# A two-layer transformer step in fp32: the first layer's modulation products move from VectorE to TensorE, and x is loaded first

## The chip, the cores and the metric

The kernel runs on one core of a Trainium2 chip. The metric is the device time of one execution in microseconds (us); the time of a kernel is the median over several runs. TensorE (PE) does matrix products, VectorE (DVE) and ScalarE (ACT) elementwise work and reductions, GpSimd (POOL) a few small powers, and SyncE (SP) issues the loads and stores.

## The reference, cut to what matters

The model has two layers, each with an attention half and an MLP half. Two streams of 128 tokens (context and latent) pass through the same weights; the model width is 2048. A conditioning vector per stream gives six vectors of 2048 per layer (shift, scale and gate of either half), and shift and scale have to be known before the first product of a half.

```python
def modulation(cvec, w_ada_l, b_ada_l):
    m = jax.nn.silu(cvec) @ w_ada_l + b_ada_l          # 2048 x 12288 weights per layer
    return jnp.split(m[:, None, :], N_MOD, axis=-1)

for l in range(DEPTH):                                  # DEPTH = 2
    sh_a, sc_a, gt_a, sh_m, sc_m, gt_m = modulation(...)
    h = rms_norm(x, g_pre_a) * (1.0 + sc_a) + sh_a
    o = attention(h @ w_in[l]) @ w_out[l]               # w_in 2048 x 4608, w_out 2048 x 2048
    x = x + gt_a * rms_norm(o, g_post_a)
    h = rms_norm(x, g_pre_m) * (1.0 + sc_m) + sh_m
    x = x + gt_m * rms_norm(jnp.square(jax.nn.relu(h @ w_up[l])) @ w_down[l], g_post_m)
```

## The kernel before

All weights stream once from HBM through SBUF, in tiles of 128 x 2048 fp32 (1 MB) called `raw`. There are five `raw` buffers (`NRAW`), and SP loads the tiles in the order in which they are used, each as soon as a buffer is free. There are three sorts of tiles:

- **Trunk tiles** (`w_in`, `w_out`, `w_up`, `w_down`). Each is split in two halves into a rounded high part `wh` (ACT, line 988) and the rest `wl` (DVE, line 989), at most three half tiles ahead (`NW`). TensorE then makes three products (`wh`·high x, `wl`·high x, `wh`·low x) per piece, 24 matmuls of 512 columns per tile of `w_in` or `w_out` (`Group.run`, lines 346 to 348).
- **Modulation tiles on TensorE** (`w_ada`, `ada_mm`, line 135). One block is one section (0 shift, 1 scale, 2 gate of the attention half; 3, 4, 5 of the MLP half) and 512 features, in four tiles. Each tile is four matmuls with 32 columns of weights. After the fourth, ACT copies the result out (`pt`, line 139), TensorE transposes it in four pieces, and DVE finishes it (`ada_post`, `mod_fin`, `gate_fin`).
- **Modulation tiles on DVE** (`w_adaT`, `dv_mul`, line 189). The transposed weights are multiplied with the broadcast conditioning vectors `sB`, one instruction for each of the two streams, with the sum in the instruction's accumulator. `load_sb` loads `sB`.

`M_A` are the eight blocks of shift and scale of the attention half, `M_M` those of the MLP half, `G_A` and `G_M` the four gate blocks of each. `DV_BLOCKS` and `PE_BLOCKS` say which engine makes which. In the first layer DVE makes `G_A`, the first two of `M_M` and `G_M` (the last in the MLP half); TensorE makes the rest.

The first layer starts with no modulation at hand. Its input product is therefore done in four **quarters** f = 0 to 3 of the 2048 input features: `make_xt(0, 0, f)` normalises, transposes, scales and shifts 512 features into `XT[f]` (high and low part), and then the `w_in` tiles of these features run for four groups of outputs ("34", "56", "78", "01"), two tiles each. Each group's sums leave PSUM after each quarter, the first time by ACT (line 776), later by DVE adding onto `stg` (line 778). The modulation of the next quarter (eight `w_ada` tiles) is woven between them, and so are some DVE tiles. Then come four tiles of the last group "2" (`c2`), the attention, and 16 tiles of `w_out`, with the rest of the modulation woven in. The attention units (`gqa`, `diff`, `na`) are stepped along between the half tiles and run to their end where a `w_out` tile needs their result.

What the code emits in this order goes through a scheduler, which sets the final order of each engine's instructions; each engine then works through its list strictly in order. `startup` loads constants on ACT's queue; `pre_norm_first` loads x on SP's queue, behind the first eight modulation tiles, and makes the row norms.

## Time and profile before

| | |
|---|---|
| median of 3 runs | 2423.8 us (2419.22 to 2427.26) |
| the profiled execution | 2420.71 us, span 2418.6 us |
| PE busy | 2301.6 us, 95% of the span |
| DVE busy | 1704.7 us, 70% |
| ACT busy | 1096.0 us, 45% |
| moved by DMA | 601.32 MB, mean 249 GB/s |
| granted TensorE clock, mean | 0.973 of full speed |

Busy time counts the union of an engine's instructions; matmuls overlap, so an engine that reads 95% can still have waited. In a chain of waits every piece is what the end waited for at that time. In a table of stretches the numbers behind the length are the busy times of PE, its weight loads, DVE, ACT and POOL with the number of instructions, then the granted clock as a share of 2.4 GHz, the share of the DMA engines' time in use, and the GB/s moved.

### The profile page before, as it was taken

The page shows a single profiled execution, that of the slowest core. Times are in us where ns is not written, and L with a number is a line of the kernel's source. Part 1 is how long each engine was busy: PE and PEld are TensorE (multiplying, and loading weights), DVE is VectorE, ACT ScalarE, POOL GpSimd, SP SyncE. Part 2 cuts the span into 40 slices and gives each one's busy share as a digit, 9 for nine tenths or more (in the row PEclk, how much of TensorE's full clock was granted, in tenths as well). Part 3 has the DMA queues.
Part 4 walks back from the last instruction along what each step waited for, and adds up shares of the span by engine and source line. Part 5 has one row for each costly group of instructions (what it writes and reads, how often), then busy time and mean ns, then how long its engine had stood idle before and what let it go on. Part 6 is the DMA issues. An engine that isn't in the chain of part 4 may idle for free.

```text
span 2418.6 us, 32541 instructions
## 1 busy us (share of the span) xinstructions
PE 2301.6 (95%) x13200; PEld 1915.8 (79%) x13200; DVE 1704.7 (70%) x2093; ACT 1096.0 (45%) x1514; POOL 33.2 (1%) x30
## 2 busy tenths in 40 slices
PE   6978988889999999999998999999999999999998
PEld 3656665659989989989976777776988988988986
DVE  2557898559888888989857687646665666565545
ACT  3523343445445434434445455546544543543543
POOL 0000000000000000000000010000000000000000
PEclk8989997999999999999998999999999999999999
DMA  9877686666777777777855766666655655665552
GB/s 366 297 304 315 252 322 232 236 265 249 293 284 292 290 284 268 290 295 282 315 221 187 265 222 235 248 223 227 225 207 212 225 208 210 215 221 209 179 187 87
DMA packets 91342, 601.32 MB, mean 249 GB/s; under 512 B 13624, under 2 KB 16056, under 8 KB 19256
## 3 DMA queue, kind: packets, MB, share of 16 engines
q1 hardware_dynamic: 90472, 598.64, 66.7%
q8 instruction: 103, 1.69, 0.3%
q10 hardware_dynamic: 720, 0.61, 0.1%
q14 instruction: 47, 0.39, 0.0%
HBM read 591.61 MB, written 7.60 MB: 248 GB/s over the span
## 4 chain that ended last, share of the span: by engine, by line
PE 87%; DVE 6%; DMA 2%; issue 2%; ACT 2%; POOL 1%; ACTq 0%; POOLq 0%; DVEq 0%
PE acc L346 17%; PE acc L347 17%; PE acc L348 17%; PE acc L382 9%; PE acc L381 9%; PE acc L380 9%; PE ada L135 2%; PE m L111 2%; DVE wl L989 2%; DVE junk L189 1%; POOL st L108 1%; DVE raw L189 1%; PE m L217 1%; DMA ngT<-ngT_in 1%; PE m L468 1%
## 5 line engine op out<-in xcount | busy, mean ns | idle before, releaser
L989 DVE TENSOR_TENSOR wl<-raw,wh 128x1024 fp32r<-128x1024 f32 x720 | 875.3, 1222 | 462.7 <-ACT wh L988 459.6
L988 ACT ACTIVATE wh<-raw 128x1024 fp32r<-128x1024 f32 x720 | 760.0, 1059 | 967.1 <-PE acc L348 592.3
L380 PE MATMUL acc<-XT,wh 128*128 128x256 f32 x2048 | 578.5, 283 | 2.8 <-ACT XT L261 2.8
L382 PE MATMUL acc<-XT,wl 128*128 128x256 f32 x2048 | 579.4, 283 | 1.6 <-DVE wl L989 1.5
L381 PE MATMUL acc<-XT,wh 128*128 128x256 f32 x2048 | 578.1, 282 | 0.3 <-DVE XT L262 0.3
L347 PE MATMUL acc<-wl,big 128*128 128x512 f32 x1280 | 509.8, 398 | 1.0 <-DVE wl L989 1.0
L346 PE MATMUL acc<-wh,big 128*128 128x512 f32 x1280 | 508.7, 401 | 1.8 <-ACT wh L988 1.8
L348 PE MATMUL acc<-wh,big 128*128 128x512 f32 x1280 | 507.6, 397 | 0.0
L380 PEld LDWEIGHTS acc<-XT,wh 128*128 128x128 f32 x2048 | 387.2, 189 | 4.3 <-ACT XT L261 3.5
L382 PEld LDWEIGHTS acc<-XT,wl 128*128 128x128 f32 x2048 | 386.7, 189 | 3.0 <-DVE wl L989 2.8
L381 PEld LDWEIGHTS acc<-XT,wh 128*128 128x128 f32 x2048 | 387.3, 189 | 1.1 <-DVE XT L262 0.8
L346 PEld LDWEIGHTS acc<-wh,big 128*128 128x128 f32 x1280 | 241.9, 189 | 68.4 <-issue 8.1
L347 PEld LDWEIGHTS acc<-wl,big 128*128 128x128 f32 x1280 | 242.9, 190 | 58.6 <-DVE wl L989 3.3
L348 PEld LDWEIGHTS acc<-wh,big 128*128 128x128 f32 x1280 | 242.7, 190 | 57.4 <-issue 1.7
L189 DVE SCALAR_TENSOR_TENSOR junk<-raw,sB 128x2048 fp8e5<-128x2048 f32 x116 | 265.1, 2285 | 32.2 <-DMA raw<-w_adaT_in 32.1
L189 DVE SCALAR_TENSOR_TENSOR raw<-raw,sB 128x2048 f32<-128x2048 f32 x116 | 264.9, 2284 | 0.1
L346 PE MATMUL acc<-wh,XT 128*128 128x512 f32 x576 | 236.0, 417 | 25.5 <-ACT XT L261 18.6
L347 PE MATMUL acc<-wl,XT 128*128 128x512 f32 x576 | 235.5, 410 | 9.5 <-DVE wl L989 9.3
L348 PE MATMUL acc<-wh,XT 128*128 128x512 f32 x576 | 232.5, 406 | 0.3 <-DVE XT L262 0.3
L346 PEld LDWEIGHTS acc<-wh,XT 128*128 128x128 f32 x576 | 111.7, 195 | 67.1 <-ACT XT L261 20.7
L347 PEld LDWEIGHTS acc<-wl,XT 128*128 128x128 f32 x576 | 112.7, 196 | 40.2 <-DVE wl L989 15.1
L348 PEld LDWEIGHTS acc<-wh,XT 128*128 128x128 f32 x576 | 111.9, 195 | 26.5 <-DVE XT L262 1.5
(132 smaller groups left out, 1200.9 us busy)
## 6 DMA issues: line engine op xcount, KB each, us to landing
raw<-w_up_in SPq DMA_DIRECT2D x128, 1024.0 KB, 4.9
raw<-w_down_in SPq DMA_DIRECT2D x128, 1024.0 KB, 4.9
raw<-w_adaT_in SPq DMA_DIRECT2D x116, 1024.0 KB, 4.9
raw<-w_in_in SPq DMA_DIRECT2D x72, 1024.0 KB, 5.9
raw<-w_ada_in SPq DMA_DIRECT2D x64, 1024.0 KB, 6.7
raw<-w_out_in SPq DMA_DIRECT2D x32, 1024.0 KB, 5.0
XT<-w_ada_in SPq DMA_DIRECT2D x12, 1024.0 KB, 6.9
sB<-crow_in SPq DMA_DIRECT2D x2, 1024.0 KB, 13.8
```

The lines of the kernel that those rows point to most:

```text
L108: pool.tensor_tensor(out, out, hf[:, 0:width], ALU.pow)
L111: pe.transpose(out, in_, ident)
L135: pe.matmul(pa[32 * g:32 * g + 32, :], sT[:, 4 * kq + g, :], raw[:, g * 512:(g + 1) * 512], start=(kq == 0), stop=(kq == 3), tile_position ...
L189: dve.scalar_tensor_tensor(o, raw, 1.0, sB[v], ALU.mult, ALU.mult, accum_out=a[:, j, v:v + 1], saturate=None if v else False)
L346: pe.matmul(a, xh, wh[:, c], start=first, stop=False)
L347: pe.matmul(a, xh, wl[:, c], start=False, stop=False)
L348: pe.matmul(a, xl, wh[:, c], start=False, stop=last)
L380: pe.matmul(a, wh[:, c], xh, start=first, stop=False)
L381: pe.matmul(a, wh[:, c], xl, start=False, stop=False)
L382: pe.matmul(a, wl[:, c], xh, start=False, stop=last)
L988: act.activation(wh, r, AF.Copy)
L989: dve.tensor_tensor(wl, r, wh.bitcast(F32), ALU.subtract)
```

## The change

1. In the first layer only `G_M` stays on DVE. `G_A` and the first two blocks of `M_M`, six blocks or 24 tiles, become `w_ada` tiles on TensorE. Nothing runs as a DVE product before the first layer's MLP half; `load_sb` moves there in the code.
2. x is loaded by `startup`, as the first thing on SP's queue.
3. The first two blocks (shift and scale of the first 512 features) are cut in halves of 256 features; a tile is then 128 x 1024 (0.5 MB, new array `w_ada0`). `make_xt` can make half a quarter, and the first `w_in` tiles run on it.
4. The four groups get five PSUM segments with bounds 0, 2, 4, 8, 12, 16 (in 128-feature steps) in place of four of equal size: one more addition of each sum onto `stg`.
5. `make_xt` of the next quarter is called ahead of the last three `w_in` tiles of the present one, and the eight modulation tiles go between its first five.

```diff
-DV_BLOCKS = [G_A + M_M[:2] + G_M, M_A + M_M[:4] + G_A[:3] + G_M]
-PE_BLOCKS = [M_A + M_M[2:], M_M[4:] + G_A[3:]]
+DV_BLOCKS = [G_M, M_A + M_M[:4] + G_A[:3] + G_M]
+PE_BLOCKS = [M_A[2:] + G_A + M_M, M_M[4:] + G_A[3:]]
...
     def startup():
+        for s in range(2):
+            x[s] = sb([P, D], "big", 5)
+            nc.sync.dma_start(x[s], xd[s])
...
-    def ada_mm(l, sec, blk, kq, raw):
+    def ada_mm(l, sec, blk, kq, raw, half=None):
+        w = 512 if half is None else 256
...
-            pe.matmul(pa[32 * g:32 * g + 32, :], sT[:, 4 * kq + g, :], raw[:, g * 512:(g + 1) * 512],
+            pe.matmul(pa[32 * g:32 * g + 32, 0:w], sT[:, 4 * kq + g, :], raw[:, g * w:(g + 1) * w],
...
-    def make_xt(l, w, f):
+    def make_xt(l, w, f, j0=0, j1=4):
...
     def pre_norm_first():
         nt[0] = sb([P, 4, 512], "big", 5)
-        for s in range(2):
-            x[s] = sb([P, D], "big", 5)
-            nc.sync.dma_start(x[s], xd[s])
...
-        def stg_done(key, ntile, after=None, S=S, nseg=4 if l == 0 else 1):
+        def stg_done(key, ntile, after=None, S=S, nseg=5 if l == 0 else 1):
...
-        gr = [Group(2, KT, xl, stg_done(key, 2, after[key]), 4 if l == 0 else None) for key in after]
+        gr = [Group(2, KT, xl, stg_done(key, 2, after[key]), [0, 2, 4, 8, 12, 16] if l == 0 else None) for key in after]
...
-            fill = ada_items(0, M_M[2:])
-            dv = dv_items(0, G_A + M_M[:2])
-            a0 = ada_items(0, M_A[:2])
-            items.extend(a0[:3])
+            fill, dv = ada_items(0, G_A + M_M), []
+            h0 = lambda h: [("ada", I["w_ada0"][sec, h, kq], (0, sec, 0, kq, h)) for sec in range(2) for kq in range(4)]
+            items.extend(h0(0)[:2])
             call(pre_norm_first)
-            items.extend(a0[3:])
-            for f in range(4):
-                call(lambda f=f: (drain_fast(), make_xt(0, 0, f)))
+            items.extend(h0(0)[2:])
+            xt = lambda *a: call(lambda: (drain_fast(), make_xt(0, 0, *a)))
+            xt(0, 0, 2)
+            m = [cg[0] for cg in cG] + [cg[1] for cg in cG]
+            ah, a1 = h0(1), ada_items(0, M_A[2:4])
+            items.extend(m[:1] + ah[:4] + m[1:2] + ah[4:] + m[2:3])
+            xt(0, 2, 4)
+            items.extend(a1[:2] + m[3:4] + a1[2:4] + m[4:5] + a1[4:6] + m[5:6] + a1[6:] + m[6:7])
+            xt(1)
+            items.extend(m[7:])
+            for f in range(1, 4):
                 ch = [c for cg in cG for c in cg[2 * f:2 * f + 2]]
-                if f == 0:
-                    ch.insert(4, ("call", load_sb))
...
                 if f < 3:
-                    weave(ch, ada_items(0, M_A[2 * f + 2:2 * f + 4]), dv[:3] if f else ())
-                    dv = dv[3:] if f else dv
+                    weave(ch[:5], ada_items(0, M_A[2 * f + 2:2 * f + 4]))
+                    items.append(ch[5])
+                    xt(f + 1)
+                    items.extend(ch[6:])
                 else:
-                    weave(ch, fill[:4], dv[:6])
-            weave(c2, fill[4:6], dv[6:10])
-            rest, fill, dv = [], fill[6:], dv[10:]
+                    weave(ch, fill[:8])
+            weave(c2, fill[8:16])
+            rest, fill = [], fill[16:]
...
-        cut = 8 if l == 0 else 40
+        cut = 0 if l == 0 else 40
...
         if l + 1 < L:
+            rest.insert(1, ("call", load_sb))
             g, m = dv_items(0, G_M), dv_items(1, M_A + M_M[:4])
...
-            weave(rest[2:118], [], dv)
+            weave(rest[4:119], [], dv)
```

At the start, SP's queue of the kernel before (`big` is x):

```order
L975 DMA raw<-w_ada_in 128x2048 x8
L268 DMA big<-xp_in 128x2048
L268 DMA big<-xs_in 128x2048
L975 DMA raw<-w_in_in 128x2048 x2
L975 DMA raw<-w_ada_in 128x2048 x2
```

and of the changed kernel:

```order
L116 DMA big<-xp_in 128x2048
L116 DMA big<-xs_in 128x2048
L988 DMA raw<-w_ada_in 128x1024 x8
L988 DMA raw<-w_in_in 128x2048
L988 DMA raw<-w_ada_in 128x1024 x4
L988 DMA raw<-w_in_in 128x2048
```

The first `w_in` tile stands behind two x tiles and eight half tiles (6 MB), where it stood behind 10 MB.

DVE's list of the kernel before where the second quarter hands over to the third (`st_88` is the sum of a modulation block, `mod` its result, `XT_105` the third quarter's input, `junk` and `raw` the two halves of a DVE product):

```order
L152 TENSOR_REDUCE st_88<-m 128x8
L189 SCALAR_TENSOR_TENSOR junk,aacc<-raw,sB_89 128x2048
L168 SCALAR_TENSOR_TENSOR mod_0_75<-st_88,baT 128x4 x2
L189 SCALAR_TENSOR_TENSOR raw,aacc<-raw,sB_90 128x2048
L169 TENSOR_TENSOR mod_0_75<-mod_0_75,ngT 128x4 x2
L989 TENSOR_TENSOR wl<-raw,wh 128x1024
L254 TENSOR_SCALAR big<-m,mod_0_75,mod_1_76 128x128 x4
L262 TENSOR_TENSOR XT_105<-big,XT_105 128x4x128
```

and of the changed kernel at the same place (the third quarter's input is `XT_109` there):

```order
L157 TENSOR_REDUCE st_88<-m 128x8
L174 SCALAR_TENSOR_TENSOR mod_0_75<-st_88,baT 128x4 x2
L175 TENSOR_TENSOR mod_0_75<-mod_0_75,ngT 128x4
L248 TENSOR_SCALAR big<-big,st_139 128x512
L1002 TENSOR_TENSOR wl<-raw,wh 128x1024 x2
L175 TENSOR_TENSOR mod_0_75<-mod_0_75,ngT 128x4
L259 TENSOR_SCALAR big<-m,mod_0_75,mod_1_76 128x128 x2
L1002 TENSOR_TENSOR wl<-raw,wh 128x1024
L782 TENSOR_TENSOR stg<-stg,acc 128x512 x4
L1002 TENSOR_TENSOR wl<-raw,wh 128x1024
L259 TENSOR_SCALAR big<-m,mod_0_75,mod_1_76 128x128 x2
L267 TENSOR_TENSOR XT_109<-big,XT_109 128x4x128
```

The two DVE products between the modulation's steps are gone, and splits and additions of tiles that still belong to the present quarter stand there.

TensorE's list of the kernel before during `w_out`, where the normed output of `diff` for the first stream (`tmp`) is transposed:

```order
L346 MATMUL acc<-wh,big 128x512
L347 MATMUL acc<-wl,big 128x512
L348 MATMUL acc<-wh,big 128x512
L111 MATMUL m<-cs,tmp 128x128 x2
L607 MATMUL m<-kT,qT 128x256
L111 MATMUL m<-cs,tmp 128x128 x2
```

and of the changed kernel:

```order
L349 MATMUL acc<-wh,big 128x512
L350 MATMUL acc<-wl,big 128x512
L351 MATMUL acc<-wh,big 128x512
L140 MATMUL ada<-raw,sT 32x512 x8
L111 MATMUL m<-cs,tmp 128x128 x3
L611 MATMUL m<-kT,qT 128x256
```

Two modulation tiles (eight matmuls) now stand ahead of the transposes, on the engine that waits there.

## Rows read from the trace of the kernel before

**Rows 1.** Stretches: length; busy PE, PEld, DVE, ACT, POOL; clock, DMA share, GB/s.

```profile
0.00:34.80 34.80, 13.38 (x76) 3.42 (x76) 4.79 (x24) 9.74 (x25) 1.36 (x6) 0.88 0.95 389
34.80:96.80 62.00, 58.05 (x277) 41.35 (x278) 24.75 (x35) 35.45 (x49) 0.09 (x1) 0.96 0.87 349
96.80:174.80 78.00, 64.44 (x274) 42.96 (x274) 54.73 (x73) 25.37 (x33) 0.00 (x0) 0.90 0.80 286
174.80:243.90 69.10, 58.39 (x278) 41.86 (x278) 49.29 (x69) 21.05 (x25) 0.00 (x0) 0.92 0.76 303
243.90:304.70 60.80, 58.13 (x258) 41.05 (x258) 50.62 (x78) 21.42 (x35) 4.63 (x2) 0.96 0.68 253
304.70:346.90 42.20, 35.29 (x152) 25.27 (x151) 38.29 (x66) 15.53 (x25) 2.44 (x1) 0.88 0.84 318
346.90:470.80 123.90, 104.67 (x462) 71.33 (x460) 96.19 (x166) 48.06 (x116) 6.02 (x2) 0.85 0.63 229
470.80:522.80 52.00, 52.00 (x237) 38.02 (x236) 23.14 (x32) 21.89 (x32) 0.56 (x1) 1.00 0.77 294
522.80:541.00 18.20, 11.97 (x83) 4.07 (x82) 13.22 (x35) 13.01 (x33) 2.54 (x3) 0.91 0.81 313
541.00:1504.00 963.00, 948.31 (x5656) 825.48 (x5657) 813.10 (x918) 458.31 (x600) 9.30 (x7) 0.99 0.71 266
```

**Rows 2.** Chain of waits at the start: start us, length us, what.

```profile
17.55 9.76 DMA big<-xp_in
...
32.63 0.74 DVE big L254 x2
...
34.81 1.22 PE acc L346 x2
```

**Rows 3.** Timeline of the start and first quarter: start us, length us, engine, line, instruction.

```profile
22.37 1.07 PE L135 MATMUL ada<-raw,sT 128*32 128x512 f32 x8 [1.43 <-DMA raw<-w_ada_in]
...
24.86 1.07 PE L135 MATMUL ada<-raw,sT 128*32 128x512 f32 x8 [1.43 <-DMA raw<-w_ada_in]
...
26.70 1.12 PE L111 MATMUL m<-cs,pt 128*128 128x128 f32 x4 [0.78 <-ACT pt L139]
...
28.28 0.24 DVE L169 TENSOR_TENSOR mod<-mod,ngT 128x4 f32<-128x4 f32 x2
...
45.04 0.39 PE L347 MATMUL acc<-wl,XT 128*128 128x512 f32 x1
...
45.27 0.40 PE L348 MATMUL acc<-wh,XT 128*128 128x512 f32 x1
```

**Rows 4.** Chain of waits from the second to the third quarter.

```profile
167.00 2.21 DVE junk L189 x2
...
169.43 2.06 issue
...
174.85 0.79 PE acc L346
```

**Rows 5.** Waits of PE, 34.8 to 304.7 us: total us, times, longest us.

```profile
PE acc L346 <- ACT XT L261: 15.8, 3, 8.3
```

**Rows 6.** DVE groups, 0 to 541 us: count, busy us, mean ns of one, idle before.

```profile
L189 DVE SCALAR_TENSOR_TENSOR raw<-raw,sB 128x2048 f32<-128x2048 f32 x24 | 54.8, 2284 | 0.1
...
L778 DVE TENSOR_TENSOR stg<-stg,acc 128x512 f32<-128x512 f32 x48 | 32.3, 684 | 27.2 <-PE acc L348 27.0
```

**Rows 7.** Timeline of PE: two modulation tiles in the midst of `w_out` products.

```profile
513.24 1.92 PE L135 MATMUL ada<-raw,sT 128*32 128x512 f32 x16
515.10 1.19 PE L346 MATMUL acc<-wh,big 128*128 128x512 f32 x4
```

**Rows 8.** Chain of waits in `c2`, 304.7 to 346.9 us, shares by line.

```profile
by line: DVE junk L189 15.6%; DVE raw L189 10.5%; PE acc L348 8.6%; DVE wl L989 8.0%; PE acc L347 7.6%; issue 7.1%; PE acc L346 6.9%; POOL st L108 5.8%; PE m L502 4.6%; PE m L111 3.8%; DVE big L451 3.3%; DVE st L421 2.8%; ACT big L450 2.6%;
```

**Rows 9.** Chain of waits during the first `w_out` tiles.

```profile
413.92 4.67 DMA raw<-w_ada_in
...
424.40 2.21 DVE junk L189 x2
```

More of the change, by code (lines that the diff above doesn't have):

```diff
@@ L138, in ada_mm, with ada_post @@
             pt = sb([P, 512], "pt")
-            act.activation(pt, pa, AF.Copy)
-            fast.append(ada_post(l, sec, blk, pt))
+            act.activation(pt[:, 0:w], pa[:, 0:w], AF.Copy)
+            fast.append(ada_post(l, sec, blk, pt, 0 if half is None else 2 * half, w // P))
     gcs = {}
     made = set()
-    def ada_post(l, sec, blk, pt):
+    def ada_post(l, sec, blk, pt, j0, nj):
         yield
         m = psm()
-        for j in range(4):
+        for j in range(nj):
             tr(m[:, j * P:(j + 1) * P], pt[:, j * P:(j + 1) * P])
         yield
-        red = st1[:, 0:8].rearrange("p (j v) -> p j v", v=2)
-        dve.tensor_reduce(red, m.rearrange("p (j g c) -> p j c g", g=4, c=32)[:, :, 0:2, :], AX.X, ALU.add)
+        red = st1[:, 0:2 * nj].rearrange("p (j v) -> p j v", v=2)
+        dve.tensor_reduce(red, m[:, 0:nj * P].rearrange("p (j g c) -> p j c g", g=4, c=32)[:, :, 0:2, :], AX.X,
+                          ALU.add)
         if sec in (2, 5):
@@ L241, in make_xt @@
             if s == 0:
-                dve.tensor_scalar(xn, x[s][:, c], r, None, ALU.mult)
+                dve.tensor_scalar(xn[:, cn], x[s][:, c], r, None, ALU.mult)
             else:
-                act.activation(xn, x[s][:, c], AF.Copy, scale=r)
+                act.activation(xn[:, cn], x[s][:, c], AF.Copy, scale=r)
             m = psm()
-            for j in range(4):
-                k = 4 * f + j
+            for j in range(j0, j1):
                 tr(m[:, j * P:(j + 1) * P], xn[:, j * P:(j + 1) * P])
             step = 2 if f == 0 else 4
-            for j in range(4):
+            for j in range(j0, j1):
                 k = 4 * f + j
@@ L257, in make_xt @@
                 if (j + 1) % step == 0:
-                    j0 = j + 1 - step
-                    tv = t[:, j0 * P:(j + 1) * P].rearrange("p (j q) -> p j q", j=step)
-                    hi = XT[f][:, j0:j + 1, 0, s * P:(s + 1) * P]
+                    i = j + 1 - step
+                    tv = t[:, i * P:(j + 1) * P].rearrange("p (j q) -> p j q", j=step)
+                    hi = XT[f][:, i:j + 1, 0, s * P:(s + 1) * P]
                     act.activation(hi, tv, AF.Copy)
-                    dve.tensor_tensor(XT[f][:, j0:j + 1, 1, s * P:(s + 1) * P], tv, hi.bitcast(F32), ALU.subtract)
+                    dve.tensor_tensor(XT[f][:, i:j + 1, 1, s * P:(s + 1) * P], tv, hi.bitcast(F32), ALU.subtract)
     def pre_norm_first():
         nt[0] = sb([P, 4, 512], "big", 5)
-        for s in range(2):
-            x[s] = sb([P, D], "big", 5)
-            nc.sync.dma_start(x[s], xd[s])
         for s in range(2):
@@ L336, in run @@
                             for _ in range(2)]
-            q, i0 = divmod(self.cnt, self.seg)
-            end = i0 + len(steps) == self.seg
+            q, i0 = self.q, self.cnt - self.segs[self.q]
+            seg = self.segs[q + 1] - self.segs[q]
+            end = i0 + len(steps) == seg
             for s in range(2):
@@ L342, in run @@
                     for i, (kt, wh, wl) in enumerate(steps):
-                        first, last = i0 + i == 0, i0 + i == self.seg - 1
+                        first, last = i0 + i == 0, i0 + i == seg - 1
                         c = slice(n * 512, (n + 1) * 512)
@@ L353, in run @@
                 self.acc = None
+                self.q += 1
         def left(self):
-            return self.seg - self.cnt % self.seg
+            return self.segs[self.q + 1] - self.cnt
     class UpGroup:
@@ L868, in trunk @@
                 rest.append(("call", load))
-        cut = 8 if l == 0 else 40
+        cut = 0 if l == 0 else 40
         nf = (len(fill) - TAIL) * cut // len(rest) // 2 * 2
-        weave(rest[:cut], fill[:nf], dv)
+        if cut:
+            weave(rest[:cut], fill[:nf], dv)
         weave(rest[cut:], fill[nf:], tail=TAIL)
@@ L931, in trunk @@
         if l + 1 < L:
+            rest.insert(1, ("call", load_sb))
             g, m = dv_items(0, G_M), dv_items(1, M_A + M_M[:4])
             dv = [x for i in range(16) for x in m[3 * i:3 * i + 3] + g[i:i + 1]]
-            weave(rest[:2], [])
-            weave(rest[2:118], [], dv)
+            weave(rest[:4], [])
+            weave(rest[4:119], [], dv)
             call(lambda: drain_dv())
             call(lambda l=l: layer_consts(l + 1))
-            items.extend(rest[118:])
+            items.extend(rest[119:])
         else:
@@ L1003, in trunk @@
         if it[0] == "ada":
-            l, sec, blk, kq = it[2]
+            l, sec, blk, kq, *half = it[2]
             r = raws.pop(ci)
-            ada_mm(l, sec, blk, kq, r)
+            ada_mm(l, sec, blk, kq, r, *half)
             state["live"] -= 1
@@ L1078, in _layout @@
     g["w_ada"] = _f(np.stack([wa[l][b].reshape(4, P, 2048) for l in range(L) for b in PE_BLOCKS[l]]))
+    g["w_ada0"] = _f(np.stack([wa[0, sec, 0].reshape(4, P, 4, 2, 256).transpose(3, 0, 1, 2, 4).reshape(2, 4, P, 1024)
+                               for sec in range(2)]))
     wt = v["w_ada"].reshape(L, D, 6, 4, 4, P).transpose(0, 2, 3, 4, 5, 1)
```

20 lines of the change are left out of this document (10 added, 10 removed).

## The prediction

> **What bounds the kernel now.** I read the table of stretches first, since the page's 95% for PE is a mean over very different parts. The MLP half from 541 us on keeps PE busy in 948 of 963 us at a clock of 0.99 [rows 1]; the change hardly touches it. The first 541 us are another matter: a start of 34.8 us, four quarters of the input product (62.0, 78.0, 69.1 and 60.8 us), `c2` (42.2), the first eight `w_out` tiles with the attention (123.9), the last eight (52.0) and a tail (18.2) [rows 1].
>
> To see how much of this is waiting I set against it what TensorE must do. One 512-column product follows the other after 45.27 - 45.04 = 0.23 us [rows 3], so a `w_in` or `w_out` tile of 24 costs 5.6 us. Two modulation tiles in the midst of other products cost 515.10 - 513.24 = 1.86 us [rows 7], 0.93 each. The last eight `w_out` tiles check this: 8 x 5.6 and four modulation tiles (3.7) are 48.5 of the 52.0 us, and the transposes and gate products fill the rest; PE is busy all the time there at full clock [rows 1]. The four quarters together take 269.9 us for 32 x 5.6 = 179, 28 x 0.93 = 26, and some 10 for transposes and first attention pieces: 215. So about 55 us of the quarters are stall or half clock (1.2 in place of 2.4 GHz); the granted clock of the second is 0.90.
>
> The chains of waits say why. Between the second and third quarter TensorE has nothing to do: DVE has a 2.21 us product of the modulation, then another (the row "issue" of 2.06 us is the second, on which the next step in DVE's order stands), ahead of the scale that the new quarter needs, and the first product comes only at 174.85 us [rows 4]. Three such hand-overs cost PE 15.8 us directly [rows 5], and the clock falls in them. In `c2` the DVE products alone are 15.6 + 10.5 = 26.1% of the chain [rows 8]. During the attention they are less: one of 2.21 us, and one load of a modulation tile that the chain waits 4.67 us for [rows 9], while DMA moves only 229 GB/s [rows 1]: the five `raw` buffers are held.
>
> **The change part by part.** *Start.* The last of eight modulation tiles is used at 24.86 us, 2.49 us after the one before it, and both waited for their load [rows 3]; x lands behind them, at 17.55 + 9.76 = 27.31 us [rows 2], and the chain runs through it. After the change x stands first and four tiles' worth follow, so six in place of eight must land before the last product of the first half block: 24.86 - 2 x 2.49 = 19.9 us. From there: product, copy and transposes 26.70 + 1.12 - 24.86 = 3.0, small DVE steps up to 28.28 + 0.24, another 0.7 [rows 3], scaling to first product 34.81 - 32.63 = 2.2 [rows 2]. That is 25.8 us in place of 34.8: **-9**. What x itself needs (27.3 to 32.6 us before) then lies under the loads. Bounds: -9, and +1 if the half tiles come no faster than whole ones (below).
>
> *Quarters.* TensorE gets 36 tiles' worth of modulation here in place of 28 (+7.4) and some transposes (+1.5): 224 us of work. The hand-over is covered by the last three tiles of the running quarter, 16.8 us of products, against the 7.9 us from the first of the two DVE products to the first new product before (167.00 to 174.85 [rows 4]) and some 3 us ahead of them for the modulation's copy and transposes. The wait for `wl` behind DVE products is gone with them. For what stays I go by the first quarter, the one without DVE products: 62.0 us for 44.8 + 7.4 + about 2.5, so 7 us, of which the hand-over at its end is about half. So 8 for the first (it now begins in a slow clock earlier) and 4.5 for each of the others: 21.5. Sum 246 in place of 270: **-24**. Bounds: stall 12 (-34) to 40 (-6). The fifth segment costs 16 additions of 0.68 us on DVE [rows 6], 11 us, against 24 x 2 x 2.28 = 110 us of products that leave it [rows 6]: hidden. DMA has to bring 16 tiles, 16.8 MB, per quarter of 58 us, 290 GB/s, less than the first quarter shows (349) [rows 1].
>
> *c2.* Six more modulation tiles, 5.6 + 0.7 for transposes. Away goes up to 26.1% of 42.2 = 11 us; behind it stand splits and attention steps, so I take 8 of the 11: **-2**. Bounds -5 and +6.
>
> *First eight `w_out` tiles.* Again six tiles more, +6.3. Away go the 2.2 and the late load of 4.7 [rows 9]; since PE waits less, part of the half clock (granted 0.85 [rows 1], so 30% of 123.9 us at 1.2 GHz) goes too, 4; and about half of the new products stand ahead of transposes for which PE waits anyway, as in front of `tmp`: 3. Sum **-8**. The waits of the attention's own steps (power on POOL, softmax) stay. Bounds -20 and +6.
>
> *Last eight and tail.* Here PE has no slack, so added work counts in full: six tiles and transposes, +6.6. And DMA becomes tight: 8 + 10 tiles, x again and four tiles kept for the end, about 23 tiles or 24 MB. The best rate of the stretches is 389 GB/s [rows 1], which gives 62 us, the first quarter's 349 gives 69; I take 63, near the start's rate because these loads wait for nothing but buffers: **+11**. The tail gets two tiles (1.9) and as much waiting for their loads: **+4**. Bounds together +8 and +21.
>
> *Rest.* The load of `sB` (2 MB) moves to `c2` and the constants of the second layer move from `w_out` to the MLP's start, on SP's queue ahead of some `w_up` tiles. Five buffers are 28 us of products; I take 0, and up to +3 if that cover fails. Two of the MLP's tiles lose their DVE companion: 0.
>
> Sum: -9 - 24 - 2 - 8 + 11 + 4 = -28 against the profiled execution of 2420.7 us: **2393 us**. That execution lies 3 us (0.13%) under the median of the runs, so the forecast may stand 3 us low.
>
> **The rivals.** *Waits are filled better.* The quarters keep 12 us of stall (-9.5), the attention's waits take all of the added products (-12), the last `w_out` tiles run at TensorE's pace (-4.5): 2367 us. For it speaks that PE waits in the attention are many; against it that its list is fixed and a product helps only where it stands.
>
> *The attention does not care for DVE's products.* Then `c2` and the first `w_out` tiles keep their lengths and get 6.3 each in place of -2 and -8: +22, 2415 us, no change that can be told (a measurement of this kernel can tell about 0.3%, 7 us). For it: DVE products hardly show in the chain of the first `w_out` tiles, and POOL and softmax steps do. Against: 26% in `c2` [rows 8].
>
> *The early start does not come.* If each half tile needs the 2.49 us of a whole one [rows 3], ten loads stand before the first scale, 24.86 + 2 x 2.49 = 29.8, and the first product comes at 35.7 us, not 25.8: 2403 us. Against it: whole tiles follow each other at 2.49 us with five under way, 421 GB/s, so the path looks full, not slow to start. The Trainium skill (DMA: Bandwidth & Descriptors, section Bandwidth) speaks for this rival: its rule is to batch loads to at least 1 MiB for three quarters of the peak rate, and here sixteen loads become half as large. No run here shows 0.5 MB tiles yet; by that rule the sum would be nearer 2403, by the rows nearer 2393.
>
> *Slower: products in order behind late loads.* TensorE takes its list in order. After the change ten pairs of modulation tiles stand in `c2` and the first `w_out` tiles between attention steps, and each waits for its load while the five buffers are held by `w_out` tiles that wait for the attention. The one such wait in the chain cost 4.67 us [rows 9]. If all ten cost that, it is +46.7: 2440 us. It decides, past 0.3%, from 8 of the 10 pairs on. Against it: DVE products held buffers too and are gone, and DMA has room there (229 GB/s).
>
> **How the numbers follow.** Forecast 2393 (2378 to 2406) 0.56; better filled 2367 0.13; attention unmoved 2415 0.13; no early start 2403 0.10; slower 2440 0.08. The range 2368 to 2416 leaves out the slower rival, about half of the best one and the upper end of the unmoved attention, 0.19 together. Faster by over 0.3% are the forecast, the best one, the late start and a third of the unmoved attention: 0.83; within 0.3% the rest of that one: 0.09; slower 0.08.
>
> **What would show it.** First `w_in` product near 26 us; the quarters' end near 272 us; no wait of PE for `XT` above 2 us between quarters; no DVE product before the MLP; the last eight `w_out` tiles longer than 58 us with DMA near 390 GB/s; first `w_up` product near 513 in place of 541 us. Wrong it would be if the quarters stay at 65 us or more each (then something other than DVE's products held them), if the stretch of the attention grows, or if the MLP half moves by more than 5 us.

## The result, and the profile after

The changed kernel takes **2355.07 us** (median of 4 runs, 2352.7 to 2357.56) against 2422.47 us of the kernel before in the same comparison: a ratio of 0.972, 95% interval 0.970 to 0.9741, or 67 us less. The forecast was 2393 us, some 30 us less, so the sign is right and the size is not; the time lies 13 us under the low end of the range. The profiled execution's span is 2354.4 us (2418.6 before). Where one run is given below, a difference of a few us says little: the four runs of the kernel after span 5 us, those of the kernel before 8.

The table of stretches of the kernel after, with the same columns and the same places in the program as [rows 1]: start, four quarters, `c2`, first eight `w_out` tiles, last eight, tail, and the MLP's first part.

```profile
0.00:26.70 26.70, 8.90 (x72) 3.06 (x72) 4.52 (x23) 11.02 (x30) 1.31 (x6) 0.97 0.93 360
26.70:98.10 71.40, 66.51 (x347) 42.88 (x347) 35.27 (x59) 33.68 (x50) 0.00 (x0) 0.96 0.84 330
98.10:158.00 59.90, 57.40 (x272) 38.85 (x272) 35.24 (x55) 20.82 (x27) 0.00 (x0) 1.00 0.81 297
158.00:212.70 54.70, 54.70 (x274) 39.09 (x273) 32.59 (x46) 20.12 (x25) 0.00 (x0) 1.00 0.83 317
212.70:272.30 59.60, 58.75 (x296) 41.21 (x294) 41.84 (x74) 30.17 (x41) 2.66 (x2) 1.00 0.76 291
272.30:309.30 37.00, 37.00 (x201) 25.95 (x199) 21.36 (x48) 16.70 (x28) 1.64 (x1) 1.00 0.85 329
309.30:412.40 103.10, 100.09 (x548) 64.98 (x546) 55.78 (x124) 48.67 (x117) 2.01 (x2) 1.00 0.80 302
412.40:467.70 55.30, 54.52 (x272) 38.77 (x271) 21.91 (x32) 20.40 (x31) 0.29 (x1) 1.00 0.84 327
467.70:491.90 24.20, 15.38 (x104) 4.90 (x102) 14.32 (x39) 14.46 (x36) 1.97 (x4) 0.86 0.91 357
491.90:1448.80 956.90, 940.16 (x5658) 824.99 (x5659) 813.79 (x922) 458.61 (x601) 9.38 (x7) 0.99 0.73 269
```

From the second quarter to the last `w_out` tile the clock reads 1.00 in every stretch; before it read 0.85 to 0.96 in all but the last of them. In the first eight `w_out` tiles DVE is busy for 55.8 us in place of 96.2. Set beside the forecast:

| stretch | before, us | after, us | change | forecast |
|---|---|---|---|---|
| start | 34.8 | 26.7 | -8.1 | -9 |
| four quarters | 269.9 | 245.6 | -24.3 | -24 |
| `c2` | 42.2 | 37.0 | -5.2 | -2 |
| first eight `w_out` tiles | 123.9 | 103.1 | -20.8 | -8 |
| last eight | 52.0 | 55.3 | +3.3 | +11 |
| tail | 18.2 | 24.2 | +6.0 | +4 |
| from the first `w_up` product to the end | 1877.6 | 1862.5 | -15.1 | 0 |
| span | 2418.6 | 2354.4 | -64.2 | -28 |

Two rows carry what was missed: the attention (13 us) and the part of the kernel that the change was said not to touch (15 us). `c2` and the last eight tiles bring 3 and 8 more.

The chain of waits at the start of the kernel after (start us, length us, what), which answers [rows 2]:

```profile
1.65 9.39 DMA tmp<-consts_in
...
12.53 3.87 ACT tmp L276 x13
...
19.35 3.07 PE ada L140 x32
...
25.71 0.95 ACT wh L1001
...
26.70 2.08 PE acc L349 x4
```

x's load is no longer in it. The load of the constants and ACT's row sums of x (the pieces of `tmp` at line 276) stand ahead of the transposes now, and behind them the last modulation products run without a wait (32 in 3.07 us): all half tiles have landed.

Waits of PE in the four quarters of the kernel after (26.7 to 272.3 us; total us, times, longest us), which answer [rows 5]:

```profile
PE acc L349 <- ACT wh L1001: 4.0, 4, 2.9
PE m L111 <- ACT pt L144: 3.9, 6, 0.7
PE acc L350 <- DVE wl L1002: 2.3, 6, 0.9
```

The wait for `XT`, 15.8 us before, does not appear.

The 15 us behind the first `w_up` product are not a wait that went. This is one stretch of `w_down`, all its 384 products (`big` holds their weights operand), in the table of stretches for these products alone; the columns are length, PE busy with the number, clock, DMA share, GB/s. Before:

```profile
2131.30:2220.60 89.30, 89.26 (x384) 1.00 0.60 214
```

and after:

```profile
2071.20:2158.30 87.10, 87.10 (x384) 1.00 0.62 220
```

The same products at the same full clock, one after the other without a gap, take 89.26 / 384 = 232.4 ns each before and 87.10 / 384 = 226.8 ns after. The kernel has 3840 products with `big` as weights: 3840 x 5.2 ns (means over the whole traces, 232.4 and 227.2) = 20 us, of which 384, 2 us, lie in the first layer's `w_out`.

### The profile page after: what moved, and what is told of

It reads as the page before. It is cut to its first block, busy times and chain, and to the rows that moved or that the text cites. A ratio compares the mean times of both kernels' runs of the same rounds, so it can differ in the third digit from the quotient of the medians.

```text
span 2354.4 us, 33079 instructions
## 1 busy us (share of the span) xinstructions
PE 2281.3 (97%) x13480; PEld 1905.2 (81%) x13480; DVE 1613.0 (69%) x2028; ACT 1101.0 (47%) x1525; POOL 25.6 (1%) x30
## 4 chain that ended last, share of the span: by engine, by line
PE 87%; DVE 5%; DMA 3%; ACT 2%; issue 2%; POOL 1%; SPq 0%; ACTq 0%; POOLq 0%; DVEq 0%
PE acc L349 16%; PE acc L350 16%; PE acc L351 16%; PE acc L386 10%; PE acc L385 10%; PE acc L384 10%; PE ada L140 3%; PE m L111 2%; DVE wl L1002 2%; DMA raw<-w_adaT_in 2%; PE m L472 1%; POOL st L108 1%; PE m L223 1%; DVE raw L195 1%; DVE junk L195 0%
## 5 line engine op out<-in xcount | busy, mean ns | idle before, releaser
L349 PE MATMUL acc<-wh,big 128*128 128x512 f32 x1280 | 502.2, 395 | 0.0
L350 PE MATMUL acc<-wl,big 128*128 128x512 f32 x1280 | 499.9, 391 | 1.7 <-DVE wl L1002 1.7
L351 PE MATMUL acc<-wh,big 128*128 128x512 f32 x1280 | 498.2, 390 | 0.0
L349 PE MATMUL acc<-wh,XT 128*128 128x512 f32 x576 | 231.0, 411 | 6.8 <-ACT wh L1001 4.0
L195 DVE SCALAR_TENSOR_TENSOR junk<-raw,sB 128x2048 fp8e5<-128x2048 f32 x92 | 210.5, 2288 | 33.1 <-DMA raw<-w_adaT_in 32.7
L350 PE MATMUL acc<-wl,XT 128*128 128x512 f32 x576 | 230.4, 400 | 2.4 <-DVE wl L1002 2.3
L351 PE MATMUL acc<-wh,XT 128*128 128x512 f32 x576 | 228.4, 397 | 0.0
L195 DVE SCALAR_TENSOR_TENSOR raw<-raw,sB 128x2048 f32<-128x2048 f32 x92 | 210.3, 2286 | 0.0
L349 PEld LDWEIGHTS acc<-wh,XT 128*128 128x128 f32 x576 | 108.6, 190 | 48.7 <-ACT wh L1001 11.3
L351 PEld LDWEIGHTS acc<-wh,XT 128*128 128x128 f32 x576 | 109.0, 189 | 24.6 <-issue 0.2
```

The costliest lines, as they stand in the source:

```text
L195: dve.scalar_tensor_tensor(o, raw, 1.0, sB[v], ALU.mult, ALU.mult, accum_out=a[:, j, v:v + 1], saturate=None if v else False)
L349: pe.matmul(a, xh, wh[:, c], start=first, stop=False)
L350: pe.matmul(a, xh, wl[:, c], start=False, stop=False)
L351: pe.matmul(a, xl, wh[:, c], start=False, stop=last)
```

## Experiments: the products that became faster without being touched

`startup` now takes x's buffers first, and `big` is their name: the five buffers moved from byte 133568 of a partition's SBUF to 94528, ahead of `XT`. The first theory was that this place sets the pitch (the time from the start of one product to the start of the next). Two runs changed only the place.

**x1**: the kernel before with x's buffers taken first (its loads and all else stay).

```diff
     def startup():
+        for s in range(2):
+            x[s] = sb([P, D], "big", 5)
...
         for s in range(2):
-            x[s] = sb([P, D], "big", 5)
             nc.sync.dma_start(x[s], xd[s])
```

> The kernel before with one thing changed: the two x tiles are allocated at the start of startup, so that the five buffers named big lie below tmp and XT in SBUF, where the changed kernel has them; x is still loaded where it was, and no instruction is added or moved. Theory A (the place in SBUF of the weights operand decides the pitch of a product): the 3840 products that take big as weights follow each other at 227 ns in place of 232, and the time falls by 3840 x 5.2 ns = 20 us, to about 2403 us. Rival B (the unchanged later stages are shorter for a reason of the new order): pitch 232 and no change, 2422 us.

Measured: 2402.99 us, ratio 0.9921 (0.9899 to 0.9943). From the first `w_up` product on, 1861.8 us as in the kernel after (all columns of [rows 1]):

```profile
542.70:2404.50 1861.80, 1827.98 (x11110) 1604.27 (x11110) 1349.09 (x1528) 884.54 (x1148) 15.62 (x15) 0.99 0.65 239
```

**x2**: the kernel after with `cT`, `tmp` and `XT` taken ahead of `big`, so that `big` lies at its old place.

```diff
     def startup():
+        cT = sb([P, 2, KT], "cT")
+        svf = sb([P, 512], "tmp", NTMP)
+        new_xt()
         for s in range(2):
             x[s] = sb([P, D], "big", 5)
...
-        cT = sb([P, 2, KT], "cT")
...
-        svf = sb([P, 512], "tmp", NTMP)
...
-        call(new_xt)
+        if l:
+            call(new_xt)
```

> The changed kernel with the buffers cT, tmp and XT allocated ahead of big, so that big lies where it lay before; the instructions and their order are those of the changed kernel. Theory A: pitch 232 ns for the products with big as weights and 20 us more than the changed kernel, about 2375 us. Rival B: pitch 227 and 2355 us.

Measured: 2374.16 us, ratio 0.9806 (0.9782 to 0.983), 1877.2 us from the first `w_up` product on, pitch 232.4 ns. With x1 this shows that the placement makes the 15 us, in either kernel.

**x3 to x6**: the kernel after with 128, 384, 64 and 192 unused bytes ahead of `big` (for x3, `sb([P, 32], "pad")` as the first line of `startup`), to see which property of the place matters.

> The changed kernel with 128 bytes per partition left free below big. big then starts at an address that leaves 448 when divided by 512, as in the kernel before, but stays in its new area; XT leaves 64. If the remainder decides, products with big as weights are back at 232 ns and the time is near 2375 us; if the area decides (below or above some address, or the neighbours), they stay at 227 and 2355 us.

> The same with 384 bytes: big leaves 192 and XT leaves 320, which is what big leaves in the changed kernel. If remainder 320 is what makes a product fast, the 1728 products with XT as weights fall from 232 to 227 ns (9 us) and those of big go to some other value; if the area decides, big stays at 227 and XT at 232.

> The changed kernel with 64 bytes of unused SBUF a partition ahead of big: big and XT then leave 128 and 0 in place of 64 and 192 of 256 bytes. If 64 alone is fast: products with big as weights at 232.5 ns, those with XT as weights at 232.5, total near 2374 us. If only 192 is slow: 227 for both, total 2350 to 2355 us.

> The changed kernel with 192 unused bytes ahead of big: big and XT leave 0 and 128 of 256 bytes. If 64 alone is fast: 232.5 ns for both, total near 2374 us. If only 192 is slow: 227 for both, total 2350 to 2355 us.

Measured, one run each: 2367.64, 2372.21, 2356.23 and 2348.88 us; pitches in the table below. x3 and x4 fitted a rule by the place alone (64 of 256 fast, 192 slow). x5 and x6 fitted neither of the two answers foreseen: two more pitches came up, and the `w_up` products, whose weights (`wh`) had not moved, became faster.

**x7**: 128 unused bytes ahead of all streaming buffers (`raw`, `wh`, `wl`, `big`, `XT`), so that every place changes and no distance between them does.

> The changed kernel with 128 unused bytes ahead of all streaming buffers: raw, wh, wl and big then leave 192 of 256 bytes where they left 64, XT leaves 64 in place of 192. If the weights operand's own place sets the pitch: products with big as weights 232.5 ns, with XT 228, total near 2370 us. If its place relative to the moving operand (wh, wl) sets it: big stays at 227, XT at 232.5, total near 2355 us.

Measured: 2358.01 us (one run), 227.3 ns with `big` at 192, the slow place of x3 and x4, and 232.6 ns with `XT` as weights at 64, their fast one. The rule by the place alone falls. One `w_down` stretch of x7, as above:

```profile
2072.54:2159.40 86.86, 86.81 (x383) 1.00 0.62 220
```

What all runs agree on is the distance from the moving operand to the weights operand (the byte address of the weights in a partition less that of the moving operand), modulo 256. Means over the consecutive products of a trace, in ns, gaps of more than about two products left out (in `w_in`, `w_out` and `w_down` the moving operand is `wh` or `wl`, 512 columns; in `w_up` `wh` or `wl` are the weights and `XT` moves, 256 columns):

| kernel | `big`: distance, ns | `XT` as weights: distance, ns | `w_up`: distance, ns |
|---|---|---|---|
| before | 128, 232.4 | 128, 232.5 | 128, 119.6 |
| after | 0, 227.2 | 128, 232.5 | 128, 119.9 |
| x3 | 128, 232.5 | 0, 228.0 | 0, 120.5 |
| x4 | 128, 232.5 | 0, 228.1 | 0, 120.6 |
| x5 | 64, 233.3 | 192, 229.3 | 64, 117.0 |
| x6 | 192, 229.1 | 64, 233.3 | 192, 117.7 |
| x7 | 0, 227.3 | 128, 232.6 | 128, 120.0 |
| y1 | 0, 227.2 | 192, 229.4 | 64, 116.6 |
| y2 | 0, 227.2 | 128, 232.6 | 128, 119.7 |
| y3 | 0, 227.2 | 192, 229.7 | 64, 116.8 |

x1 (`big` at 0, 227.3 ns) and x2 (128, 232.4) fit the same table.

Three more runs were made to try this reading on new places.

**y2**: 64 unused bytes ahead of all streaming buffers: each place is new (128 of 256, `XT` 0), each distance that of the kernel after.

> The changed kernel with 64 unused bytes ahead of all streaming buffers: raw, wh, wl and big leave 128 of 256, XT leaves 0. All distances are those of the changed kernel (big 0, XT 128), all absolute places are others. If distance sets the pitch: big 227, XT as weights 232.5, w_up products 120 ns, total near 2355 us. If the absolute place of the moving operand sets the w_up pitch (XT at 0 was fast): 117 ns, total near 2337 us.

Measured: 2357.3 us (one run), and the pitches of the kernel after. The distance sets the pitch, not the place, in `w_up` too. One `w_up` stretch, its 768 products alone, of y2:

```profile
2158.80:2251.60 92.80, 91.56 (x768) 1.00 0.52 182
```

**y1**: the kernel after with 64 unused bytes between `big` and `XT`, the best pair of distances that these buffers gave.

```diff
             nc.sync.dma_start(x[s], xd[s])
+        sb([P, 16], "pad")
         cT = sb([P, 2, KT], "cT")
```

> The changed kernel with 64 unused bytes between big and XT, so raw, wh, wl and big stay where they are (64 of 256) and XT leaves 0 in place of 192. Distance of the weights operand from the moving one, modulo 256: big 0, XT as weights 192, wh against XT 64. By the pitches of the runs before at these distances: big 227 ns as now, XT as weights 229.4 (now 232.5), w_up products 117.0 (now 119.9). 6144 w_up products x 2.9 ns is 18 us, and up to 1728 x 3.1 = 5 us in w_in: total near 2334 us (2330 to 2340). If the pitches of big and XT are bound together in another way (big slows when XT leaves 192): 2350 us or more.

Measured: **2333.74 us**, ratio to the kernel before 0.9646 (0.9621 to 0.967), the fastest version here, and at the number worked out from the pitches. The same `w_up` stretch of y1:

```profile
2137.40:2226.40 89.00, 87.75 (x768) 1.00 0.54 190
```

**y3**: the kernel before with x's buffers first and the same 64 bytes.

> The kernel before with x's buffers (big) taken first and 64 unused bytes between big and XT: the placement of y1_best in the kernel before, nothing else of the change. x1 (big alone) gave 2403 us. If w_up products go from 119.6 to 117.0 ns here too: 6144 x 2.6 = 16 us less than x1 and some 3 from w_in, 2382 to 2388 us. Otherwise 2400 us or more.

Measured: 2391.79 us (one run), 11 us less than x1 in place of 15 to 21, so the forecast was missed by some 4 us, which is within the 6 us that x1's own runs span. The pitches came as foreseen. The traces show where some of their gain went: from the first `w_up` product on y3 takes 1852.6 us and x1 1861.8, 9 us less in place of 16, and a wait for the split on DVE grew. PE's wait for `wl` in `w_up` in that part (total us, times, longest us) in x1 and in y3:

```profile
PE acc L383 <- DVE wl L990: 3.3, 5, 1.3
```

```profile
PE acc L384 <- DVE wl L991: 9.7, 9, 2.4
```

That is 6 us more. Why DVE is late there stays open.

## Experiments: why the attention became 21 us shorter

Three theories: (A) the DVE products stand in DVE's list between the attention's own steps, and TensorE waits and loses its clock behind them; (B) the buffers that their tiles hold and their loads delay the `w_out` tiles; (C) another part of the change did it (start, hand-over, constants on SP's queue).

**s2**: the kernel before with part 1 of the change alone (`load_sb` stays where it was); **s1**: the kernel after with part 1 alone undone. The cut is s2's; s1 turns the same lists and weaves back, with `load_sb` ahead of them.

```diff
-DV_BLOCKS = [G_A + M_M[:2] + G_M, M_A + M_M[:4] + G_A[:3] + G_M]
-PE_BLOCKS = [M_A + M_M[2:], M_M[4:] + G_A[3:]]
+DV_BLOCKS = [G_M, M_A + M_M[:4] + G_A[:3] + G_M]
+PE_BLOCKS = [M_A + G_A + M_M, M_M[4:] + G_A[3:]]
...
-                    weave(ch, fill[:4], dv[:6])
-            weave(c2, fill[4:6], dv[6:10])
+                    weave(ch, fill[:8], dv[:6])
+            weave(c2, fill[8:16], dv[6:10])
...
-        cut = 8 if l == 0 else 40
+        cut = 0 if l == 0 else 40
```

> The kernel before with part 1 of the change alone: the six blocks become TensorE tiles, placed in the order of the changed kernel; old start, old four segments, old hand-over, x at its old SBUF place. Theory A: the first eight w_out tiles fall to 100 to 106 us with a clock near 1.00, the last eight grow to 55 to 57 us, the quarters fall by 10 to 20 us (part of -28; the rest is the hand-over), start unchanged at 34.8, the MLP half unchanged within 2 us; total near 2393 us. Rival C: the stretch stays above 115 us, and the total is 2405 us or more.

> The changed kernel with the six modulation blocks (G_A and the first two of M_M) put back as VectorE products in the places they had in the kernel before; new start, five segments, new hand-over and the fast SBUF place of x are kept. The question is why the first eight w_out tiles with the attention fell by 21.3 us (123.9 to 102.6) where -8 was forecast. Theory A, VectorE's products stand in the attention's order on VectorE and the half clock follows from the waits: the stretch goes back to 115 us or more with a granted clock under 0.93, the last eight tiles come back to about 52 us, total near 2375 us. Rival C, the new start, the hand-over or the constants' other place in SP's queue made the gain: the stretch stays within 4 us of 102.6 less the 6 us of TensorE work it loses, so 96 to 103 us, and the total is near 2350 us.

Measured: s2 2384.67 us, ratio 0.9846 (0.9822 to 0.9869); s1 2398.76 us, 0.99 (0.9879 to 0.9921). Stretches of s2 (all four quarters, then first and last eight `w_out` tiles):

```profile
34.70:278.00 243.30, 231.46 (x1114) 163.43 (x1114) 134.67 (x208) 103.37 (x140) 2.78 (x3) 0.97 0.78 299
315.20:418.70 103.50, 100.30 (x541) 64.88 (x539) 55.72 (x125) 49.08 (x116) 3.01 (x2) 0.98 0.77 293
418.70:476.00 57.30, 56.52 (x278) 38.95 (x277) 22.20 (x33) 20.53 (x32) 0.53 (x1) 1.00 0.85 331
```

and the first eight `w_out` tiles of s1:

```profile
344.60:465.10 120.50, 100.48 (x458) 68.70 (x456) 95.23 (x166) 48.48 (x116) 4.07 (x2) 0.87 0.63 226
```

Part 1 alone makes the whole gain in the attention (103.5), and undoing it gives all but 3 us back (120.5, clock 0.87). C falls. Two things in s2 came otherwise than foreseen: the quarters fell by 26.6 us and not by 10 to 20, so that its total is 8 us under the number foreseen, and from the first `w_up` product on it took 1881.7 us, 4 us more than the kernel before; the cause of these 4 us was not sought. s1's total came out 24 us over the number foreseen, since its quarters (272 us) and `c2` (45.1) grew as well, which the expectation had left out.

**s3**: the kernel before with the 24 tiles' DVE products narrowed to 128 of 2048 columns, loads and buffers kept.

```diff
...
+            wd = 128 if l == 0 and sec != 5 else D
-            dve.scalar_tensor_tensor(o, raw, 1.0, sB[v], ALU.mult, ALU.mult, accum_out=a[:, j, v:v + 1],
-                                     saturate=None if v else False)
+            dve.scalar_tensor_tensor(o[:, 0:wd], raw[:, 0:wd], 1.0, sB[v][:, 0:wd], ALU.mult, ALU.mult,
+                                     accum_out=a[:, j, v:v + 1], saturate=None if v else False)
```

> The kernel before, with the 24 tile products of VectorE in the first layer's start, quarters, c2 and w_out narrowed from 2048 to 128 columns, their loads kept (so the sums of these six blocks leave out 15 of 16 columns). Takes VectorE's time away (2.28 to some 0.2 us each, 48 products, about 100 us of which some 59 in c2 and w_out) and leaves loads and buffers as they are. Theory A (VectorE's time in the attention's order): the first eight w_out tiles fall from 123.9 to 112 us or less, clock over 0.92. Rival B (the buffers that these tiles hold and their loads ahead of w_out tiles): they stay within 5 us of 123.9. Quarters fall by 10 us or more under either.

Measured: 2366.62 us (one run). Its `c2` and first eight `w_out` tiles:

```profile
282.80:315.30 32.50, 31.95 (x151) 23.49 (x150) 26.12 (x62) 15.49 (x26) 1.64 (x1) 1.00 0.71 273
315.30:417.40 102.10, 94.39 (x454) 67.25 (x452) 56.27 (x149) 47.32 (x114) 2.01 (x2) 0.92 0.80 313
```

All tiles are still loaded into the same buffers, DVE's time is gone (56.3 us busy in place of 96), and the stretch falls by 21.8 us, `c2` by 9.7; the clock, 0.92, only touches what was foreseen. That is theory A, and B is not needed for it. B is not excluded altogether, since a shorter product also gives its buffer back sooner; but SP's waits for buffers that DVE's products release hardly changed in this stretch (7.8 us before, 6.1 in s3). DVE's products in the stretch of the kernel before, 19 in all (groups of DVE, columns as in [rows 6]):

```profile
L189 DVE SCALAR_TENSOR_TENSOR raw<-raw,sB 128x2048 f32<-128x2048 f32 x10 | 22.8, 2281 | 0.0
L189 DVE SCALAR_TENSOR_TENSOR junk<-raw,sB 128x2048 fp8e5<-128x2048 f32 x9 | 20.5, 2278 | 0.0
```

43.3 us of 124. Where they bite is read from PE's waits in the same stretch of the kernel before (total us, times, longest us):

```profile
PE m L111 <- DVE tmp L660: 9.7, 2, 6.2
PE m L111 <- DVE big L484: 2.9, 1, 2.9
PE m L111 <- DVE big L627: 2.0, 1, 2.0
```

and of the kernel after:

```profile
PE m L111 <- DVE tmp L664: 1.3, 1, 1.3
PE m L111 <- DVE big L488: 1.1, 1, 1.1
PE m L111 <- DVE big L631: 0.6, 1, 0.6
```

The steps waited for are the attention's own (they take 0.3 to 0.4 us each). 11.6 us of direct waits go, and the clock comes from 0.85 to 1.00. DVE's products reach these steps in two ways. They stand ahead of them in DVE's list: two, from 410.27 to 414.9 us, ahead of the step of line 627, and one ahead of line 107 below. And they lengthen the power on POOL (line 108), for which the step that writes `tmp` waits. The wait for line 484 has no product in the 6 us ahead of it; it is not explained by this. Before the wait of 6.2 us in the kernel before (timelines of DVE and POOL):

```profile
424.32 2.28 DVE L189 SCALAR_TENSOR_TENSOR junk<-raw,sB 128x2048 fp8e5<-128x2048 f32 x1
426.53 0.17 DVE L107 TENSOR_SCALAR st<-st 128x4 f32<-128x4 f32 x1
426.64 2.29 DVE L189 SCALAR_TENSOR_TENSOR raw<-raw,sB 128x2048 f32<-128x2048 f32 x1
426.84 2.96 POOL L108 TENSOR_TENSOR st<-st,hf 128x4 f32<-128x4 f32 x1 [31.88 <-DVE st L107]
429.83 1.13 DVE L660 SCALAR_TENSOR_TENSOR tmp<-m,st,bcs 128x128 f32<-128x128 f32 x4 [0.89 <-POOL st L108]
```

and the same steps in the kernel after:

```profile
373.81 0.17 DVE L107 TENSOR_SCALAR st<-st 128x4 f32<-128x4 f32 x1
374.13 1.01 POOL L108 TENSOR_TENSOR st<-st,hf 128x4 f32<-128x4 f32 x1 [18.83 <-DVE st L107]
375.17 1.13 DVE L664 SCALAR_TENSOR_TENSOR tmp<-m,st,bcs 128x128 f32<-128x128 f32 x4 [1.18 <-POOL st L108]
```

The same power takes 2.96 us beside a product and 1.01 without one. The stretch has two of them, and POOL is busy for 6.02 us in the kernel before, where both run beside a product, for 4.07 in s1, where one does, and for 2.01 in s3 and in the kernel after, where none runs beside a long one. So about 4 of the 9.7 us of waits for `tmp` come through POOL (an estimate from these busy times).

**s4**: the kernel before with the same DVE products on two resident tiles, 24 MB of loads left out; **inconclusive**.

```diff
...
+            if raw is None:
+                o = sb([P, D], "junk", 1, FP8)
+                dve.scalar_tensor_tensor(o, sB[1 - v], 1.0, sB[v], ALU.mult, ALU.mult, accum_out=a[:, j, v:v + 1],
+                                         saturate=False)
...
```

> The kernel before, with the same 24 tile products of VectorE made on two tiles that lie in SBUF anyway (the broadcast conditioning vectors) in place of loaded tiles, so 24 MB of loads and their buffers are left out, and with them these six blocks' true results; VectorE's time stays. Theory A: the first eight w_out tiles stay within 6 us of 123.9. Rival B: they fall to 112 us or less.

Measured: 2388.96 us (one run); the first eight `w_out` tiles take 96.7 us, which reads like B. But without a load to follow, the scheduler put the products elsewhere. DVE's products alone, in first and second quarter, third and fourth, `c2`, and the first eight `w_out` tiles of s4:

```profile
34.60:101.30 66.70, 11.49 (x10) 0.93 0.85 342
101.30:190.30 89.00, 50.48 (x44) 0.85 0.55 198
190.30:311.80 121.50, 41.20 (x36) 0.93 0.66 246
311.80:344.60 32.80, 6.82 (x6) 1.00 0.69 264
344.60:441.30 96.70, 0.00 (x0) 0.98 0.53 185
```

None is left in the attention (43.5 us before), so the run does not hold DVE's time still there and cannot speak on B. It agrees with A in another place: the second quarter, into which 50 us of them went, takes 89 us in place of 78.

**h1**: the kernel after with part 5 alone undone (`make_xt` behind the last tile of the quarter, the modulation tiles woven between all eight).

```diff
+            items.extend(m[7:])
             xt(1)
-            items.extend(m[7:])
...
-                    weave(ch[:5], ada_items(0, M_A[2 * f + 2:2 * f + 4]))
-                    items.append(ch[5])
+                    weave(ch, ada_items(0, M_A[2 * f + 2:2 * f + 4]))
                     xt(f + 1)
-                    items.extend(ch[6:])
```

> The changed kernel with part 5 alone undone: the next quarter's input is made after the last w_in tile of the present quarter, and the eight modulation tiles are woven between all eight of them, as in the kernel before; everything else as changed. As forecast (the three tiles ahead cover a hand-over of about 8 to 11 us): the four quarters grow from 245.6 us by 3 x 4 to 3 x 8 us, to 258 to 270, clock 0.95 or less in them, total 2367 to 2380 us. Rival (with no product of VectorE in it the hand-over is short anyhow; the kernel before with part 1 alone had quarters of 243.3 us in all): 246 to 256 us, total 2356 to 2365 us.

Measured: 2365.71 us, ratio 0.9757 (0.9737 to 0.9777), about 10 us over the kernel after. Its four quarters together, and the wait that comes back in them:

```profile
27.20:278.80 251.60, 235.92 (x1183) 162.76 (x1183) 145.59 (x233) 105.37 (x140) 2.66 (x2) 0.99 0.79 303
```

```profile
PE acc L349 <- ACT XT L266: 6.4, 3, 2.7
```

251.6 against 245.6 us: 6 us of hand-over, as the rival said, not 12 or more. Another 3 us are lost in the first eight `w_out` tiles (105.8), for which no cause was sought.

## Why the prediction was wrong in size

- **Start: right in the number** (-8.1 for -9), and the rival of the late start fell: the first product came at 26.70 us, not 35.7. The path is not the one that was added up, so the close fit is in part luck: the forecast let the last half tile's load set the time and put x's own work under the loads, while the chain of the kernel after runs through the load of the constants (to 11.05 us) and ACT's row sums of x, and the half tiles wait for these. In the first 26.7 us the DMA engines moved 360 GB/s, with modulation in half tiles; the kernel before moved 380 in the same time and 389 in its whole start [rows 1], with whole tiles. The Trainium skill (DMA: Bandwidth & Descriptors, section Bandwidth) advises batches of at least 1 MiB; with several loads under way, tiles of 0.5 MB cost little here, and the measurement decides. But the gain did not last: the first quarter grew from 62.0 to 71.4 us, which holds the second half block's modulation now (PE x347 in place of x277). Its end lies at 98.1 us, where it lay at 96.8. h1 (part 1 with the new start, halves and segments, no new hand-over) reaches the first `w_up` product at 501.7 us, s2 (part 1 alone) at 499.2.
- **Quarters: right as a sum** (-24.3 for -24). Its terms, taken by quarter, give some 67, 60, 60 and 60 us (an estimate); 71.4, 59.9, 54.7 and 59.6 came. The hand-over's part was taken too large: s2 has 243.3 us of quarters without the new hand-over, so taking DVE's products out of DVE's list did nearly all, and the new hand-over is worth 6 us (h1).
- **`c2`: sign right, 3 us short.** The share of DVE's products in the chain (26%, 11 us) was a good price there: s3 shows 9.7 us, where 8 were taken, and the added work cost 4.5 (37.0 against s3's 32.5), not 6.3.
- **First eight `w_out` tiles: the step that failed.** The working priced the removed products by what showed in the chain of waits, one product of 2.21 us and one load of 4.67 [rows 9], plus 4 us of clock: 11. s3 measures 21.8 for their removal alone. The chain names at each time what ended last; a product that delays another step shows there as that step, or as TensorE's half-speed products behind it. The POOL power is the plain case: it stands in the chain with 2.97 us where 1.01 is its own. The forecast let this wait stay ("power on POOL, softmax"); POOL's busy time in the stretch fell from 6.02 to 2.01 us. The rows that had the size were DVE's own, 43 us of products in a stretch of 124, the granted clock of 0.85, and PE's waits: 15.6 of 19.1 us of direct waits are for DVE. The added work was also priced too high: 103.1 us against s3's 102.1, so about 1 us in place of 3.3. The rival "the attention does not care for DVE's products" is refuted. "Waits are filled better" had the number for this stretch (-20), but by luck: it let the waits take up the added products, which can bring no more than these 3.3 us over the forecast, while the gain came from the products that left.
- **Last eight tiles: the step that failed the other way.** They were given 63 us as DMA-bound. They took 55.3, with PE busy in 54.5 and 327 GB/s: 327 x 55.3 = 18 MB came in, not 24, since the earlier stretch loaded more (302 GB/s for 229) and the tail takes some. TensorE's pace set the time, as the rival "waits are filled better" had it; s2, at the old pitch, has 57.3.
- **Tail: right** (+6.0 for +4).
- **Rest: 0 was wrong by 15 us, by a mechanism that was not in the list.** The forecast read one pitch (0.23 us [rows 3]) and took it as a property of the product. The lines of the diff that take x's buffers first moved five buffers in SBUF; x1, x2, x7 and y2 show that the pitch follows the distance between the two operands' places. "The MLP half moves by more than 5 us" stood there as a sign of being wrong, and it was one.
- **Slower rival: did not come.** PE's wait for modulation tiles does not appear in the first eight `w_out` tiles after the change.

Of the 64 us of span, s2 accounts for 37.7 by part 1 alone, h1 for 9.4 by the new hand-over, and the placement for 15 to 20 (x1, x2); start and segments add nothing that these runs can tell.

## What to carry to other kernels

Where the chain of waits runs through many short steps of an engine, work that leaves this engine can be worth far more than the chain shows of it: in this attention half of the 43 us of products came out, 21.8 us, where the chain showed 2.2 of a product. Where the chain shows the products themselves, as in `c2`, its share was a good price (11 us shown, 9.7 measured). Look also at what runs on another engine beside such a product: POOL's power took three times as long there. Before calling a part of a kernel untouched, look whether an added or moved allocation shifts the buffers that its products read, and compare the pitch of wait-free products, which one row of a stretch tells. If several versions are compared, hold the placement still, or its share (15 to 20 us of 2420 here) is credited to the edit.

## What the runs showed of the hardware

The pitch of 128x512 fp32 products at full clock was 227.2 to 228.1 ns, 229.1 to 229.7, 232.4 to 232.6 or 233.3 ns when the weights operand lay 0, 192, 128 or 64 bytes (modulo 256) above the moving operand in SBUF; that of 256-column products was 120.5 to 120.6, 117.7, 119.6 to 120.0 or 116.6 to 117.0 ns at these distances. All kernels of the table agree on it, and two of them (x7, y2) speak against the place of one operand alone; why the distance matters was not tried, nor any distance that is not a multiple of 64.

A power of 128x4 elements on POOL (line 108) took 1.01 us with no DVE instruction of over 1 us beside it, and 2.96 to 3.06 us when a DVE product of 2.28 us had started 0.1 to 0.2 us before it; it then ended about 0.9 us behind the product (all three of this size in the first 541 us of the kernel before, and the two of s1 that run beside a product). In s3, where the product takes 0.29 us, it took 1.01 and 1.04 us beside one. No run was made to find out why.
